# An mLSTM and HGRN2 step on one core: the keys of the four memory heads are turned by VectorE and DMAs instead of TensorE

## The chip, the core and the metric

The kernel runs on one core of a Trainium2 chip. It is one program of some 23,800 instructions over TensorE (PE in the profile; its weight loads are PEld), VectorE (DVE), ScalarE (ACT), GpSimd (POOL) and SyncE (SP, which issues nearly all DMAs). Each engine works through its own instructions in their order and waits for others by semaphores. The metric is the device time of one execution in microseconds (us): the lower, the better.

## What is computed

The reference is one step of a streaming encoder: 512 frames of a new stream and 32 frames of a running one, width 1024, in float32. A projection `x @ w_in` feeds two branches, an mLSTM with four heads of width 512 and an HGRN2 with eight heads of width 128; both are merged by gates and projected out. The part that the change touches is the mLSTM's new matrix memory, a product over time of weighted keys and values, for which the keys are needed with time on the partitions:

```python
qm = jnp.einsum('bthd,hde->bhte', ch, w_qm)
km = jnp.einsum('bthd,hde->bhte', ch, w_km) * (M_HD ** -0.5)
...
w_last = jnp.exp(b[..., -1:] - b + ig - m_last[..., None])
decay = jnp.exp(m_prev[..., -1] - m_last)
C_new = decay[..., None, None] * C + jnp.einsum('bhs,bhse,bhsd->bhed', w_last, v, k)
n_new = decay[..., None] * n + jnp.einsum('bhs,bhsd->bhd', w_last, k)
```

## The kernel before

Every large matrix product is made of three: each float32 operand is split into a high part (`...h`, a rounding copy on ACT) and a low part (`...l`, the rest, a subtraction on DVE), and PE adds up high times high, low times high and high times low. Activations lie with features on the 128 partitions and 544 frames (512 + 32) along the free side; PE takes them in two halves of 272. A weight block of 128x512 arrives by one DMA from SP, is split by one ACT cast (L205) and one DVE subtraction (L206), and then serves 12 matmuls of 128x272, a block.

The heads of the memory run one after the other (loop from L1656): `stage_k` (L970) projects the keys to four tiles `kf` of 128 features by 544 frames and splits them; `stage_q` (L997) does the queries; `stage_scores` (L1025) multiplies both, masks (`dm`) and splits the scores (`sh`, `sl`); then `mchain` (L1119) turns keys and values so that time lies on the partitions, and multiplies them to the new memory. `mchain` is a generator: at each `yield n` the `Pump` (L671) runs n half blocks of the projection `w_in` in between, so that PE has matmuls while ACT and DVE prepare operands. For heads 1 to 3 these come from a pairwise scheme (`Two`) with seven blocks of 12 matmuls: `a11, a12` and so on are plain weights (`wa...`), `s1` to `s4` sums of weights (`ws...`, an addition on DVE at L509 ahead of the split). With heads 1, 2 and 3 the first pair is 20, 24 and 28, and its blocks come in the order a11 (ahead of the scores), a12, s2, s1, s3, then a11 of the next pair, a22 and so on. `Pump.load` (L702) issues the raw weights' DMAs, `Pump.prepare` (L736) writes a block's sums and splits three blocks ahead (AHEAD = 3); with `behind` set, they are issued after the instruction that it names.

In `mchain`, for each of the four blocks b of 128 frames, PE turns the key tiles by four transposes against an identity (L1129) into `kt`; ACT writes the weighted keys' high part `kwh` (L1133), DVE the low part `kwl` (L1134). Three copies of the last stream's 32 frames, `ksm`, are turned the same way (L1144) and give `kws` (L1149, L1151). KTGAP (L45) holds the half blocks ahead of each. The values follow with four transposes per block (`vt`, L1176), split to `vh` (L1179) and `vl` (L1180). For head 3, SP also writes the parts to memory (`kv_d`, L1218).

The order on PE is the order in which the code is written (`manual_schedule`). On ACT, DVE, POOL and SP a scheduler places the instructions ahead of time, by readiness and priority (`high_priority` puts the weighted keys first; `issue_after(x)` keeps an instruction behind x); on the chip that order is fixed, and each queue stops at an instruction that waits.

Of the kernel before, what the change touches and what calls it, by code (L numbers as in the profile page):

```python
# [9 lines left out]
F32 = mybir.dt.float32  # L10
# [4 lines left out]
ALU = mybir.AluOpType  # L15

P = 128
D = 1024
KD = D // P
NS = 32  # L20
NP = 512
T = NS + NP
TH = T // 2
FAR, NEAR = 48, 4
MH = 4
# [19 lines left out]
KTGAP = ((3, 2, 1, 1, 1), (4, 4, 4, 4, 4))  # L45
# [8 lines left out]
SUMSAT = (3,)  # L54
# [30 lines left out]
def hybrid_step(ctx: ExitStack, tc: tile.TileContext, a, o):  # L85
# [585 lines left out]
    class Pump:  # L671


        def __init__(self, todo, staged=False, src=a["w_in"]):
            self.src, self.rawahead = src, RAWAHEAD
            self.done, self.when, self.behind, self.staged = 0, {}, None, staged
# [25 lines left out]
        def load(self, i):  # L702
            b = self.order[i]
            if b[1]:
                need = self.loads.index(b[1][-1]) + 1
                for u, i in self.loads[self.loaded : need + self.rawahead]:
                    self.raw[u, i] = raw_piece(self.src[u][:, i * WP : (i + 1) * WP], f"wi{u}r{i}")
                self.loaded = max(self.loaded, min(need + self.rawahead, len(self.loads)))
# [252 lines left out]

    def triple(src, name, after=None):

        t = small(name, [P, KH, 3, NS], bufs=1)
        for f in range(KH):
            with tc.issue_after(after.ins) if after is not None else nullcontext():
                last = G.tensor_copy(t[:, f], src[f][:, :NS].rearrange("p (o t) -> p o t", o=1).to_broadcast([P, 3, NS]))  # L967
        return t.rearrange("p f o t -> p f (o t)"), last

    def stage_k(h):  # L970

        cs = st8[h]["cs"]
        kf, ks = [], []
        for u in range(2):
            w = st8[h]["wk"][u] if "wk" in st8[h] else weight(a["w_km"][h, u], f"wk{h}{u}", at=in_slots)
            for f in range(2):
# [11 lines left out]
                kf.append(t)  # L988
                kh, kl = slot(f"kh{h}{u}{f}", F32R), slot(f"kl{h}{u}{f}", F32R)
                S.copy(kh[:, :NP], t[:, NS:T])  # L990
                V.tensor_tensor(kl[:, :NP], t[:, NS:T], kh[:, :NP].bitcast(F32), ALU.subtract)
                ks.append((kh, kl))
        ksm, copied = triple(kf, "ksm")
        st8[h].update(kf=kf, ks=ks, ksm=ksm, copied=copied)
# [122 lines left out]
    kv_d = dr.tile([2 * NB, 2, P, VW], F32, name="kv_d")  # L1117

    def mchain(h, pump):  # L1119
# [3 lines left out]
        kf, ksm, wi = t["kf"], t["ksm"], t["wi"]  # L1123
        kw = []
        for b in range(NB):
            yield KTGAP[h > 0][b]
            pt = paux(f"kt{h}{b}")
            for f in range(KH):
                PE.transpose(pt[:, 0, f * P : (f + 1) * P], kf[f][:, NS + b * P : NS + (b + 1) * P], ident)  # L1129
            kh, kl = slot(f"kwh{h}{b}", F32R), slot(f"kwl{h}{b}", F32R)  # L1130
            wc = col[:, 10 + b, h : h + 1]
            with tc.high_priority():
                S.mul(kh[:, :HD], pt[:, 0, :], wc)  # L1133
                low = V.scalar_tensor_tensor(kl[:, :HD], pt[:, 0, :], wc, kh[:, :HD].bitcast(F32), ALU.mult, ALU.subtract)  # L1134
            if h == 0 and b in SUMSAT:
                with tc.issue_after(low.ins):
                    for k in FIRST:
                        xf[k] = xf_sums(k)
                    lower_bounds()
            kw.append((kh, kl))  # L1140
        yield KTGAP[h > 0][NB]
        pt = paux(f"kts{h}")
        for f in range(KH):
            PE.transpose(pt[: 3 * NS, 0, f * P : (f + 1) * P], ksm[:, f], ident)  # L1144

        kws = small("kws", [3 * NS, HD], F32R, bufs=1)
        wc = cols[:, 1, h : h + 1]
        with tc.high_priority():
            S.mul(kws, pt[: 3 * NS, 0, :], wc)  # L1149
            lo = slice(2 * NS, 3 * NS)  # L1150
            V.scalar_tensor_tensor(kws[lo], pt[lo, 0, :], wc[lo], kws[lo].bitcast(F32), ALU.mult, ALU.subtract)  # L1151
# [504 lines left out]
    with tc.manual_schedule(engines={mybir.EngineType.PE}):  # L1656
        for h in range(MH):
# [9 lines left out]
            if h == 0:  # L1667
                col, cols, combo = stage_cols(*rows)
                stage_decay(h)
                lower_bounds = hgrn_bounds(st8[0]["decayed"], st8[0]["masked"])  # L1670
# [525 lines left out]
```

## Time and profile before

| | us |
|---|---|
| median of three runs | 1108.1 (1108.09 to 1108.41) |
| the profiled execution | 1109.5 |
| its span, first to last instruction | 1107.8 |
| PE busy | 1098.2 |
| DVE busy | 920.7 |
| ACT busy | 713.9 |
| POOL busy | 166.8 |
| the DMA engines' share, main queue | 37.4% |

How to read it: PE's busy time is nearly the span, so what PE does not have to do shortens the step, and what PE has to wait for lengthens it, wherever in the step that is. The timeline rows in the next sections give the start (us from the span's start), the duration, the engine, the line, the operation with its output and inputs (buffer numbers left out) and how often; a bracket holds the idle time ahead and what ended it. Since instructions of one engine overlap by their latency, the pitch from one start to the next is the time that one costs in a row of them.

### The profile page before, as it was taken

Reading aid. Unit: us, or ns where it says so; the run is one execution under the profiler, and the core shown is the slowest. Engines: PE = TensorE matmul, PEld = TensorE weight load, DVE = VectorE, ACT = ScalarE, POOL = GpSimd, SP = SyncE. Lnnn points to the kernel's source line nnn. Section 1 sums busy time; section 2 is a strip of 40 time slices with the busy share of each in tenths; the row PEclk is TensorE's granted clock in tenths of the full one; section 3 lists DMA queues with packets and bytes.
Section 4 is the critical chain, followed back from the end, with each engine's and each line's share of the span. In section 5 each row is a group of like instructions: output and inputs, shape, how many; then the busy total and the mean of one; then the engine's idle time right before and its main releaser. Section 6 shows DMA issues by size and latency. Waiting matters only on the chain.

```text
span 1107.8 us, 23790 instructions
## 1 busy us (share of the span) xinstructions
PE 1098.2 (99%) x8825; PEld 1085.8 (98%) x8825; DVE 920.7 (83%) x1977; ACT 713.9 (64%) x1571; POOL 166.8 (15%) x417
## 2 busy tenths in 40 slices
PE   9999999999999999999999999999999999999998
PEld 9999999999999999999999999999999999999998
DVE  6987999676896786986898699999999888789785
ACT  6686656754666555664666478787777776445662
POOL 2212024201010110101200123322323100000000
PEclk9999999999999999999999999999999999999999
DMA  6233225332264132461656322122222353343953
GB/s 223 78 96 107 89 78 183 101 113 99 68 218 163 39 125 103 133 224 53 201 172 207 108 77 84 56 84 74 84 71 75 102 177 114 113 126 104 304 153 120
DMA packets 78044, 135.78 MB, mean 123 GB/s; under 512 B 8804, under 2 KB 16612, under 8 KB 77928
## 3 DMA queue, kind: packets, MB, share of 16 engines
q1 hardware_dynamic: 77760, 134.21, 37.4%
q8 instruction: 69, 1.13, 0.4%
q14 instruction: 47, 0.39, 0.1%
q10 hardware_dynamic: 168, 0.06, 0.0%
HBM read 109.32 MB, written 24.91 MB: 121 GB/s over the span
## 4 chain that ended last, share of the span: by engine, by line
PE 89%; DVE 7%; ACT 2%; issue 1%; DMA 1%; SPq 0%; POOL 0%; DVEq 0%; ACTq 0%
PE d L576 38%; PE ya L230 9%; PE pg L2047 4%; PE yb L230 4%; PE k L230 4%; PE q L230 4%; PE C L1098 3%; PE pl L1770 3%; PE u L356 2%; PE sc L1040 2%; PE v L230 2%; PE nm L1280 2%; PE ple L230 1%; PE d L456 1%; PE ho L1885 1%
## 5 line engine op out<-in xcount | busy, mean ns | idle before, releaser
L593 ACT COPY t<-d 128x272 f32<-128x272 f32 x126 | 47.5, 377 | 5.0 <-PE d L576 4.8
L1791 DVE TENSOR_TENSOR hkq<-hkq,hq 128x288 f32<-128x288 f32 (+1 forms) x96 | 41.5, 439 | 4.9 <-PE pl L1778 1.6
L1726 ACT COPY kmos<-hkq 128x256 f32<-128x256 f32 x56 | 23.9, 427 | 30.4 <-DVE hkq L1791 29.6
L1770 PE MATMUL pl<-hkq,kmos 128*128 128x128 f32 x224 | 38.2, 293 | 1.1 <-ACT kmos L1726 0.7
L802 DVE SCALAR_TENSOR_TENSOR cv<-ub,vec,cv 128x547 f32<-128x547 f32 x48 | 37.1, 782 | 0.4
L1770 PEld LDWEIGHTS pl<-hkq,kmos 128*128 128x128 f32 x224 | 30.9, 190 | 3.9 <-ACT kmos L1726 2.4
L1209 DVE SCALAR_TENSOR_TENSOR c<-c,wi,Cs 128x256 f32<-128x256 f32 (+1 forms) x32 | 15.1, 476 | 19.3 <-PE Cs L1207 19.2
L1098 PE MATMUL C<-vh,kwl 128*128 128x256 f32 x96 | 27.0, 281 | 0.0
L1098 PE MATMUL C<-vl,kwh 128*128 128x256 f32 x96 | 26.9, 280 | 0.0
L1098 PE MATMUL C<-vh,kwh 128*128 128x256 f32 x96 | 26.8, 279 | 0.0
L1348 DVE TENSOR_TENSOR y<-ya,y 128x272 f32<-128x272 f32 x48 | 18.8, 434 | 8.1 <-PE ya L230 8.1
L1806 DVE COPY_PREDICATED at<-lmask,pl 128x256 f32<-128x256 uint8 x56 | 24.9, 445 | 0.0
L1280 PE MATMUL nm<-vh,sh 128*128 128x256 f32 x80 | 22.9, 286 | 0.9 <-ACT y L1291 0.5
L1280 PE MATMUL nm<-vh,sl 128*128 128x256 f32 x80 | 22.5, 282 | 0.0
L1280 PE MATMUL nm<-vl,sh 128*128 128x256 f32 x80 | 22.5, 281 | 0.0
L1110 ACT COPY Co<-C 128x516 f32<-128x516 f32 x12 | 7.1, 590 | 21.0 <-PE C L1098 17.4
L1054 ACT CAST sh<-dm 128x512 fp32r<-128x512 f32 (+3 forms) x16 | 7.3, 459 | 20.4 <-DVE dm L1048 20.4
L967 POOL COPY vsm<-vt 128x96 f32<-128x96 f32 x16 | 7.4, 472 | 86.5 <-ACT vt L604 43.6
L1291 ACT COPY y<-nm 128x516 f32<-128x516 f32 x16 | 9.4, 589 | 16.9 <-PE nm L1280 16.9
L1040 PE MATMUL sc<-q,kh 128*128 128x512 f32 (+3 forms) x80 | 18.6, 321 | 0.1
L795 POOL COPY uo<-ub 128x3 f32<-128x3 f32 x16 | 6.8, 428 | 76.4 <-DVE ub L600 40.8
L1098 PEld LDWEIGHTS C<-vh,kwh 128*128 128x128 f32 x96 | 18.1, 189 | 0.0
(5761 smaller groups left out, 5196.1 us busy)
## 6 DMA issues: line engine op xcount, KB each, us to landing
ya_d<-y SPq DMA_DIRECT2D x32, 272.0 KB, 3.0
y<-ya_d SPq DMA_DIRECT2D x24, 272.0 KB, 3.6
c<-in_C SPq DMA_DIRECT2D x16, 258.0 KB, 3.7
out_Cs<-c SPq DMA_DIRECT2D x16, 258.0 KB, 2.7
out_Cp<-Co SPq DMA_DIRECT2D x15, 258.0 KB, 2.5
x<-in_xT SPq DMA_DIRECT2D x8, 272.5 KB, 4.8
ya<-ya_d SPq DMA_DIRECT2D x8, 272.0 KB, 5.1
h<-in_xT SPq DMA_DIRECT2D x8, 272.0 KB, 2.7
```

The lines of the kernel that those rows point to most:

```text
L230: PE.matmul(both[b][:m, :TH], part(w, off + k * step, m, x), xx[:, half(b)], start=(k == 0 and j == 0), stop=(k == n - 1 and j == 2),)
L576: PE.matmul(ps, ww[:, c], xx, start=(start and k == 0 and j == 0), stop=end, skip_group_check=not start,)
L593: S.copy(t, ps)
L802: last = V.scalar_tensor_tensor(cv[:, :547], ub[:, j : j + 547], vcol(V_CW + 4 * ft + j), cv[:, :547], ALU.mult, ALU.add)
L1040: PE.matmul(pn[:, 0, :n], ks[f][x][:, j * P : (j + 1) * P], qs[f][y][:, NS + j * P : T], start=(f == 0 and i == 0), stop=(f == KH - 1 and ...
L1098: PE.matmul(pn[g], kw[b][x][:, f * P : (f + 1) * P], vv[b][y][:, VS[g]], start=(b == 0 and j == 0), stop=(b == NB - 1 and j == 2),)
L1280: PE.matmul(pn[:, g, VP[g] : VP[g] + VN[g]], st[j][x][:, (i - j) * P : (i - j + 1) * P], vv[j][y][:, VS[g]], start=(j == 0 and q == 0), st ...
L1726: S.copy(km.rearrange("p (n j c) -> p n j c", j=2, c=c), view(kk, HB, ((2 * c, NA // (2 * c)), (c - HB, 2), (1, c))),)
L1770: PE.matmul(pn[:, b * P : (b + 1) * P], km[:, b * P : (b + 1) * P], view(qq, b * P, ((2 * c, P // (2 * c)), (HB + c, 2), (1, c))), start=True,
L1791: V.tensor_tensor(x, x, t, ALU.mult)
L1806: V.copy_predicated(blocks2(at[:, :NA]), twice(lmask[:, li, :P]), blocks2(pn[:, :NA]))
L2047: PE.matmul(ps, part(w, k * P, P, x), xx[:, c], start=(k == 0 and j == 0), stop=(k == KD - 1 and j == 2))
```

## The change

The 80 PE transposes of the keys and of `ksm` are taken out. Instead, DVE turns each `kf` tile in place by squares of 32 by 32 (`V.transpose` over 128x544, new function `turn`), and four DMAs per tile, each of 32 partitions by 17 by 32 numbers, write the squares to their places in a buffer `k_d` in memory, frame by frame; 16 such DMAs per head. From there `mchain` reads four blocks of 128x512 into the slots of `kwl`, and three copies of 32x512 into `kr`. ACT and DVE make `kwh`, `kwl` and `kws` from these in SBUF. All reads and splits are written at once behind the scores, ahead of the first `yield`. For heads 1 to 3, later raw weights are issued behind the last read (`ahead`), and later sums and splits of weights behind the last `kwl` (`behind`). Head 0's turns are written behind its decay. KTGAP keeps the sums of half blocks, 8 and 20, in two parts each; the `xf` sums of head 0 stand behind the first 7 of them. The copies `ksm` are made tile by tile in `stage_k`.

```diff
@@ -42,7 +42,7 @@
 PDGAP = 1
 VGAPS = (0, 0, 0, 0)
 ZN = 3
-KTGAP = ((3, 2, 1, 1, 1), (4, 4, 4, 4, 4))
+KTGAP = ((7, 1), (16, 4))
 VTGAP = ((2, 1, 1, 1, 1), (1, 1, 1, 1, 1), (1, 1, 1, 1, 1), (0, 2, 2, 1, 1))
 GAPS = (20, 20, 20, 14)
 APART = 10
@@ -51,7 +51,6 @@
 FACTORS = 0
 HOLDS = (0,)
 WV1AT = 6
-SUMSAT = (3,)
 FIRST = (0,)
 THEN = (3, 1, 2)
 SLOT = 550
@@ -673,7 +672,7 @@
 
         def __init__(self, todo, staged=False, src=a["w_in"]):
             self.src, self.rawahead = src, RAWAHEAD
-            self.done, self.when, self.behind, self.staged = 0, {}, None, staged
+            self.done, self.when, self.behind, self.ahead, self.staged = 0, {}, None, None, staged
             order, base = [], 0
             for n, e in enumerate(todo):
                 last = todo[n - 1] if n else None
@@ -703,8 +702,9 @@
             b = self.order[i]
             if b[1]:
                 need = self.loads.index(b[1][-1]) + 1
-                for u, i in self.loads[self.loaded : need + self.rawahead]:
-                    self.raw[u, i] = raw_piece(self.src[u][:, i * WP : (i + 1) * WP], f"wi{u}r{i}")
+                with tc.issue_after(self.ahead.ins) if self.ahead is not None else nullcontext():
+                    for u, i in self.loads[self.loaded : need + self.rawahead]:
+                        self.raw[u, i] = raw_piece(self.src[u][:, i * WP : (i + 1) * WP], f"wi{u}r{i}")
                 self.loaded = max(self.loaded, min(need + self.rawahead, len(self.loads)))
 
         def stage(self, n, upto):
@@ -959,18 +959,31 @@
         G.tensor_copy(wi, bc[:, T : T + NS])
         st8[h].update(dj=dj, ds=ds, wi=wi, decayed=decayed, masked=masked)
 
+    def thrice(dst, src):
+
+        return G.tensor_copy(dst, src[:, :NS].rearrange("p (o t) -> p o t", o=1).to_broadcast([P, 3, NS]))
+
     def triple(src, name, after=None):
 
         t = small(name, [P, KH, 3, NS], bufs=1)
         for f in range(KH):
             with tc.issue_after(after.ins) if after is not None else nullcontext():
-                last = G.tensor_copy(t[:, f], src[f][:, :NS].rearrange("p (o t) -> p o t", o=1).to_broadcast([P, 3, NS]))
+                last = thrice(t[:, f], src[f])
         return t.rearrange("p f o t -> p f (o t)"), last
+
+    def turn(dst, f, t):
+
+        V.transpose(t[:, :T], t[:, :T])
+        blocks = dst.rearrange("(n t) e -> t n e", t=NS)
+        for i in range(P // NS):
+            e = f * P + i * NS
+            nc.sync.dma_start(blocks[:, :, e : e + NS], t[i * NS : (i + 1) * NS, :T].rearrange("p (n e) -> p n e", e=NS))
 
     def stage_k(h):
 
         cs = st8[h]["cs"]
         kf, ks = [], []
+        ksm = small("ksm", [P, KH, 3, NS], bufs=1)
         for u in range(2):
             w = st8[h]["wk"][u] if "wk" in st8[h] else weight(a["w_km"][h, u], f"wk{h}{u}", at=in_slots)
             for f in range(2):
@@ -985,13 +998,15 @@
                     read = S.mul(t[:, half(b)], acc[b], HD**-0.5)
                 if u == 0:
                     first = read
-                kf.append(t)
                 kh, kl = slot(f"kh{h}{u}{f}", F32R), slot(f"kl{h}{u}{f}", F32R)
                 S.copy(kh[:, :NP], t[:, NS:T])
                 V.tensor_tensor(kl[:, :NP], t[:, NS:T], kh[:, :NP].bitcast(F32), ALU.subtract)
+                copied = thrice(ksm[:, u * 2 + f], t)
+                if h:
+                    turn(k_d[h], u * 2 + f, t)
+                kf.append(t)
                 ks.append((kh, kl))
-        ksm, copied = triple(kf, "ksm")
-        st8[h].update(kf=kf, ks=ks, ksm=ksm, copied=copied)
+        st8[h].update(kf=kf, ks=ks, ksm=ksm.rearrange("p f o t -> p f (o t)"), copied=copied)
         return first
 
     def stage_q(h, u):
@@ -1115,40 +1130,41 @@
         yield
 
     kv_d = dr.tile([2 * NB, 2, P, VW], F32, name="kv_d")
+    k_d = [dr.tile([T, HD], F32, name=f"k_d{h}") for h in range(MH)]
 
     def mchain(h, pump):
 
         t = st8[h]
 
-        kf, ksm, wi = t["kf"], t["ksm"], t["wi"]
+        wi = t["wi"]
         kw = []
         for b in range(NB):
-            yield KTGAP[h > 0][b]
-            pt = paux(f"kt{h}{b}")
-            for f in range(KH):
-                PE.transpose(pt[:, 0, f * P : (f + 1) * P], kf[f][:, NS + b * P : NS + (b + 1) * P], ident)
             kh, kl = slot(f"kwh{h}{b}", F32R), slot(f"kwl{h}{b}", F32R)
+            raw = kl[:, :HD].bitcast(F32)
+            read = nc.sync.dma_start(raw, k_d[h][NS + b * P : NS + (b + 1) * P, :])
             wc = col[:, 10 + b, h : h + 1]
             with tc.high_priority():
-                S.mul(kh[:, :HD], pt[:, 0, :], wc)
-                low = V.scalar_tensor_tensor(kl[:, :HD], pt[:, 0, :], wc, kh[:, :HD].bitcast(F32), ALU.mult, ALU.subtract)
-            if h == 0 and b in SUMSAT:
-                with tc.issue_after(low.ins):
-                    for k in FIRST:
-                        xf[k] = xf_sums(k)
-                    lower_bounds()
+                S.mul(kh[:, :HD], raw, wc)
+                low = V.scalar_tensor_tensor(kl[:, :HD], raw, wc, kh[:, :HD].bitcast(F32), ALU.mult, ALU.subtract)
             kw.append((kh, kl))
-        yield KTGAP[h > 0][NB]
-        pt = paux(f"kts{h}")
-        for f in range(KH):
-            PE.transpose(pt[: 3 * NS, 0, f * P : (f + 1) * P], ksm[:, f], ident)
-
+        if h:
+            pump.ahead, pump.behind = read, low
+        kr = small("kr", [3 * NS, VW], bufs=1, tag="vs")[:, :HD]
+        for i in range(3):
+            nc.sync.dma_start(kr[i * NS : (i + 1) * NS], k_d[h][:NS, :])
         kws = small("kws", [3 * NS, HD], F32R, bufs=1)
         wc = cols[:, 1, h : h + 1]
         with tc.high_priority():
-            S.mul(kws, pt[: 3 * NS, 0, :], wc)
+            S.mul(kws, kr, wc)
             lo = slice(2 * NS, 3 * NS)
-            V.scalar_tensor_tensor(kws[lo], pt[lo, 0, :], wc[lo], kws[lo].bitcast(F32), ALU.mult, ALU.subtract)
+            V.scalar_tensor_tensor(kws[lo], kr[lo], wc[lo], kws[lo].bitcast(F32), ALU.mult, ALU.subtract)
+        yield KTGAP[h > 0][0]
+        if h == 0:
+            with tc.issue_after(low.ins):
+                for k in FIRST:
+                    xf[k] = xf_sums(k)
+                lower_bounds()
+        yield KTGAP[h > 0][1]
         c0 = [eslot(f"c0{h}{f}") for f in range(KH)]
         for f in range(KH):
             nc.sync.dma_start(c0[f][:, :VW], a["C0"][h, f])
@@ -1667,6 +1683,8 @@
             if h == 0:
                 col, cols, combo = stage_cols(*rows)
                 stage_decay(h)
+                for f, t in enumerate(st8[0]["kf"]):
+                    turn(k_d[0], f, t)
                 lower_bounds = hgrn_bounds(st8[0]["decayed"], st8[0]["masked"])
             low = stage_q(h, 1)
             if h == 0:
```

**ScalarE in head 1, from the queries to the first blocks behind the scores.** `ws320h`, `wa1122h` and `wa2220h` are high parts of weights for the blocks s3, a11 of the next pair and a22; `sh` are the scores' high parts; `t1620` is a copy of block s2's result out of PSUM. Before:

```order
L205 CAST ws320h_3449<-ws320_3447 128x512
L205 CAST wa1122h_3468<-wi22r0_3310 128x512
L1016 CAST qh13_3289<-q1111_3264 128x272
L1013 COPY qf_3140<-q1110_3263 128x32
L1016 CAST qh13_3289<-q1110_3263 128x272
L1022 ACT_TABLE_LOAD
L1022 ACTIVATE silu_3296<-ident_108 1x2
L593 COPY t120_3350<-d200_3334 128x272
L205 CAST wa2220h_3495<-wi21r1_3304 128x512
L1054 CAST sh10_3384<-dm10_2958 128x512
L1054 CAST sh11_3402<-dm11_2959 128x384
L1054 CAST sh21_3368<-dm12_2960 128x256
```

and now, from the scores on:

```order
L1069 CAST sh10_3411<-dm10_2965 128x512
L1069 CAST sh11_3429<-dm11_2966 128x384
L1069 CAST sh21_3395<-dm12_2967 128x256
L1069 CAST sh21_3395<-dm12_2967 128x128
L592 COPY t1620_3538<-d200_3361 128x272
L1147 ACTIVATE kwh10_3474<-kwl10_3475,col_1348 128x512
L1158 ACTIVATE kws_3498<-kr_3494,cols_1350 96x512
L1147 ACTIVATE kwh11_3479<-kwl11_3480,col_1348 128x512
L1147 ACTIVATE kwh12_3484<-kwl12_3485,col_1348 128x512
L1147 ACTIVATE kwh13_3489<-kwl13_3490,col_1348 128x512
L204 CAST ws320h_3503<-ws320_3501 128x512
L204 CAST wa1122h_3522<-wi22r0_3337 128x512
```

The casts of the weights stood ahead of the scores and now stand behind the five weighted-key instructions, and these behind the copy of s2's result.

**VectorE in the same place.** `ql` are the queries' low parts, `vt10` a result of block a12, `ws320` the sum of weights for block s3. Before, ahead of the scores:

```order
L509 TENSOR_TENSOR ws222_3517<-ws122_3515,wi22r0_3310 128x512
L1017 TENSOR_TENSOR ql12_3257<-q1100_3230,qh12_3256 128x272
L1017 TENSOR_TENSOR ql12_3257<-q1101_3231,qh12_3256 128x272
L206 TENSOR_TENSOR ws320l_3450<-ws320_3447,ws320h_3449 128x512
L509 TENSOR_TENSOR ws422_3575<-ws222_3517,wi22r1_3466 128x512
L206 TENSOR_TENSOR wa1122l_3469<-wi22r0_3310,wa1122h_3468 128x512
L1017 TENSOR_TENSOR ql13_3290<-q1111_3264,qh13_3289 128x272
L1017 TENSOR_TENSOR ql13_3290<-q1110_3263,qh13_3289 128x272
L206 TENSOR_TENSOR wa2220l_3496<-wi21r1_3304,wa2220h_3495 128x512
L1048 TENSOR_TENSOR dm10_2958<-sc10_3370,dm10_2958 128x512
```

and now, behind them:

```order
L1070 TENSOR_TENSOR sl21_3396<-dm12_2967,sh21_3395 128x128
L1084 TENSOR_TENSOR dss_3470<-dm12_2967,dss_3470 32x32
L599 TENSOR_TENSOR vt10_3363<-d201_3362,t120_3377 128x272
L1148 SCALAR_TENSOR_TENSOR kwl10_3475<-kwl10_3475,col_1348,kwh10_3474 128x512
L1160 SCALAR_TENSOR_TENSOR kws_3498<-kr_3494,cols_1350,kws_3498 32x512
L1148 SCALAR_TENSOR_TENSOR kwl11_3480<-kwl11_3480,col_1348,kwh11_3479 128x512
L1148 SCALAR_TENSOR_TENSOR kwl12_3485<-kwl12_3485,col_1348,kwh12_3484 128x512
L1148 SCALAR_TENSOR_TENSOR kwl13_3490<-kwl13_3490,col_1348,kwh13_3489 128x512
L508 TENSOR_TENSOR ws320_3501<-wi20r0_3325,wi21r0_3329 128x512
L508 TENSOR_TENSOR ws122_3560<-wi23r0_3343,wi23r1_3345 128x512
L508 TENSOR_TENSOR ws222_3562<-ws122_3560,wi22r0_3337 128x512
L205 TENSOR_TENSOR ws320l_3504<-ws320_3501,ws320h_3503 128x512
```

The sum for s3 was made ahead of these rows (and its low part among them); now the sum stands behind the last `kwl`, and its low part behind two further sums.

**ScalarE in head 0, at the turns of the values.** `vt00` and `vt01` are PE's turned values, of which two can be held at a time; `ws24h` belongs to a later block. Before:

```order
L1133 ACTIVATE kwh03_1638<-kt03_1633,col_1344 128x512
L205 CAST wa124h_2208<-wi4r1_1714 128x512
L837 ACTIVATE z01_1670<-d330_1550 128x272
L1149 ACTIVATE kws_1678<-kts0_1673,cols_1346 96x512
L837 ACTIVATE z01_1670<-d331_1551 128x272
L1326 ACTIVATE c1_840<-c1_840,vec_84 128x544
L1179 CAST vh00_1708<-vt00_1703 128x512
L1163 CAST c0p00_1880<-c000_1681 128x516
L1163 CAST c0p01_1883<-c001_1682 128x516
L1179 CAST vh01_1731<-vt01_1726 128x512
L205 CAST ws24h_2232<-ws24_2230 128x512
```

and now:

```order
L1179 CAST c0p00_1887<-c000_1688 128x516
L1179 CAST c0p01_1890<-c001_1689 128x516
L1147 ACTIVATE kwh02_1584<-kwl02_1585,col_1348 128x512
L204 CAST ws24h_2239<-ws24_2237 128x512
L1147 ACTIVATE kwh03_1589<-kwl03_1590,col_1348 128x512
L1195 CAST vh00_1715<-vt00_1710 128x512
L1195 CAST vh01_1738<-vt01_1733 128x512
```

`vh00`, which frees the turned values' PSUM together with `vl00` on DVE, now stands behind `ws24h` and `kwh03`.

**SyncE in head 3, behind the scores.** `kv_d` is the copy of the weighted keys in memory, `s0` a load of HGRN2 state. Before, the writes to `kv_d` stood among loads of weights:

```order
L1840 DMA s0_10116<-in_S0 128x128
L173 DMA wi45r1_7831<-in_w_in 128x512
L173 DMA wi44r1_7881<-in_w_in 128x512
L1218 DMA kv_d_139<-kwh30_7753 128x512
L1218 DMA kv_d_139<-kwl30_7754 128x512
L173 DMA wi46r0_7960<-in_w_in 128x512
L1218 DMA kv_d_139<-kwh31_7805 128x512
L1218 DMA kv_d_139<-kwl31_7806 128x512
L1218 DMA kv_d_139<-kwh32_7857 128x512
L1218 DMA kv_d_139<-kwl32_7858 128x512
```

and now they share the queue with the reads of turned keys:

```order
L1144 DMA kwl30_7743<-k_d3_143 128x512
L1154 DMA kr_7762<-k_d3_143 32x512 x3
L1144 DMA kwl31_7748<-k_d3_143 128x512
L1234 DMA kv_d_139<-kwh30_7742 128x512
L1234 DMA kv_d_139<-kwl30_7743 128x512
L1858 DMA s0_9693<-in_S0 128x128
L1144 DMA kwl32_7753<-k_d3_143 128x512
L1234 DMA kv_d_139<-kwh31_7747 128x512
L1234 DMA kv_d_139<-kwl31_7748 128x512
L1858 DMA s0_10132<-in_S0 128x128
L1144 DMA kwl33_7758<-k_d3_143 128x512
L1234 DMA kv_d_139<-kwh32_7752 128x512
L1234 DMA kv_d_139<-kwl32_7753 128x512
```

The read of the last block, into `kwl33`, stands behind the writing of `kwl31`.

## The prediction

> **What bounds the kernel now.** I read the page first, for the engine that is never free, then the groups of instructions on PE, then the timeline where the change acts.
>
> ```profile
> PE 1098.2 (99%) x8825; PEld 1085.8 (98%) x8825; DVE 920.7 (83%) x1977; ACT 713.9 (64%) x1571; POOL 166.8 (15%) x417
> PE 89%; DVE 7%; ACT 2%; issue 1%; DMA 1%; SPq 0%; POOL 0%; DVEq 0%; ACTq 0%
> ```
>
> PE is busy for 1098.2 of 1107.8 us and makes up 89% of the chain that ended last. So each microsecond taken off PE is worth one, and each that PE waits costs one; nothing behind a wait is caught up, since PE has no slack to catch up with.
>
> ```profile
> L1129 PE MATMUL kt<-ident,kf 128*128 128x128 f32 x64 | 9.6, 272 | 0.0
> L1144 PE MATMUL kts<-ident,ksm 128*96 128x128 f32 x16 | 2.4, 272 | 0.0
> ```
>
> These are the 80 transposes that go. Their idle time is 0.0: PE never waited for them.
>
> **What goes.** Busy time overlaps in a pipelined engine, so I price a group of four from starts in head 1:
>
> ```profile
> 228.64 0.37 PE L576 MATMUL d<-xh,wa1220h 128*128 128x272 f32 x1
> ...
> 231.57 0.29 PE L576 MATMUL d<-xfh,ws220l 128*128 128x272 f32 x1
> 231.70 0.60 PE L1129 MATMUL kt<-ident,kf 128*128 128x128 f32 x4
> 232.05 0.37 PE L576 MATMUL d<-xfh,ws120h 128*128 128x272 f32 x1
> 232.26 0.29 PE L576 MATMUL d<-xfl,ws120h 128*128 128x272 f32 x1
> 232.39 0.28 PE L576 MATMUL d<-xfh,ws120l 128*128 128x272 f32 x1
> ...
> 233.62 0.29 PE L576 MATMUL d<-xfh,ws320h 128*128 128x272 f32 x1
> ```
>
> From 231.70 to 232.05 are 0.35 us, and the next matmul takes 0.21 instead of 0.13, so a group costs about 0.44. There are 20 groups: **8.8 us** saved, at least 20 x 0.35 = 7.0. The same splits of the keys remain on ACT and DVE.
>
> **What comes in, heads 1 to 3.** The rows of order on ACT and DVE say that block s3 (ws320 in head 1) now gets its weights behind all weighted keys, and these stand behind the copy of s2's result. The durations:
>
> ```profile
> 236.95 0.74 DVE L1134 SCALAR_TENSOR_TENSOR kwl<-kt,col,kwh 128x512 fp32r<-128x512 f32 x1
> 237.61 0.68 DVE L509 TENSOR_TENSOR ws<-ws,wi36r 128x512 f32<-128x512 f32 x1
> 238.21 0.68 DVE L206 TENSOR_TENSOR wa1136l<-wi36r,wa1136h 128x512 fp32r<-128x512 f32 x1
> ```
> ```profile
> 232.35 0.38 ACT L593 COPY t<-d 128x272 f32<-128x272 f32 x1
> 232.63 0.69 ACT L1133 ACTIVATE kwh<-kt,col 128x512 fp32r<-128x512 f32 x1
> ```
> ```profile
> 109.14 0.69 ACT L1133 ACTIVATE kwh<-kt,col 128x512 fp32r<-128x512 f32 x1 [0.51 <-PE kt L1129]
> 109.72 0.61 ACT L205 CAST wa124h<-wi4r 128x512 fp32r<-128x512 f32 x1
> 110.23 0.40 ACT L837 ACTIVATE z<-d 128x272 f32<-128x272 f32 x1
> ```
>
> On DVE a `kwl` costs 0.66 in a row, a sum 0.60; on ACT the copy 0.28, a `kwh` from PSUM 0.58, a cast from SBUF 0.51. A `kwh` from SBUF is in no row; it lies between the last two, and I take 0.57, which the five together move by 0.3 at most. In head 1, on the clock of before: s2 ends at 231.57 + 0.29 = 231.86; the copy runs to 232.2; five instructions of 0.57 bring the end of `kwh13` to 235.15; `kwl13` to 235.85; the sum to 236.55; the cast `ws320h` to 237.2. Without transposes PE asks for it at 233.62 - 0.44 = 233.2, so it waits **4.0**. Its third matmul needs `ws320l`, which stands behind two more sums (236.45 + 2 x 0.60 + 0.7 = 238.35) and is asked for at 237.5: **0.9** more. Head 1: 4.9. Behind it the splits run ahead of PE again, at about 0.6 a piece against 1.48 a block. In head 2 one `kwh` stands ahead of the copy: 4.9 - 0.57 = **4.3**.
>
> Head 3 has SP's queue in the way: the read into `kwl33` is issued behind the write of `kwl31`.
>
> ```profile
> 529.52 0.33 SPq L1218 DMA_DIRECT2D kv_d<-kwl  x1
> ```
> ```profile
> c<-in_C SPq DMA_DIRECT2D x16, 258.0 KB, 3.7
> ```
> ```profile
> DMA to landing us min/median/max: 2.3/4.2/5.5
> ```
>
> Counted from the first matmul behind the scores (228.64 in head 1): the copy ends at 3.5, `kws` and `kwh31` follow to 4.8, `kwl31` to 5.6; its write, a state load and the read are issued at 5.6, 5.95 and 6.3; at 3.7 to landing the data is there at 10.0; `kwh33` ends at 10.75, `kwl33` at 11.45, the sum at 12.15, the cast at 12.8. PE asks at 233.2 - 228.64 = 4.5. It waits 8.3, and 0.9 for the low part: **9.2**, with landings of 2.3 to 5.5 (the extremes of the `kv_d` transfers) 7.8 to 11.0.
>
> **Head 0.** Here `vt02` waits for `vl00`, and this for `kwh03` and `kwl03`.
>
> ```profile
> 113.52 0.41 PE L456 MATMUL d<-xl,wi340h 128*128 128x272 f32 x2
> 113.78 0.41 PE L456 MATMUL d<-xh,wi340l 128*128 128x272 f32 x2
> 114.05 0.66 PE L1176 MATMUL vt<-ident,vt 128*128 128x128 f32 x4
> ```
>
> Five groups earlier, PE wants `vt02` at 114.05 - 2.2 = 111.85. `ws24h`, ahead of `kwh03` on ACT, writes over `wi340h`, whose last use begins at 113.52 - 2.2 = 111.3 and ends at 111.75. Then `ws24h` 0.51, `kwh03` to 112.95; DVE has `ws24l` and a sum in between, so `kwl03` ends at 114.2 and `vl00` at 115.0. PE waits 3.1, and 0.2 at the turn of the last frames: **3.3**. The reads are no later: the last is issued behind matmuls of the scores, and some 60 matmuls at 0.13, 7.5 us, lie between the scores and `vt00`, which covers the longest landing of 5.5.
>
> **What is hidden.** 16 turns of 128x544 come on DVE, an operation in no row; the nearest is an addition of that size:
>
> ```profile
> L399 DVE TENSOR_TENSOR xu<-xh,xl 128x544 f32<-128x544 f32 x4 | 2.8, 705 | 0.0
> ```
> ```profile
> 206.51 0.69 DVE L509 TENSOR_TENSOR ws<-wi21r,wi21r 128x512 f32<-128x512 f32 x1 [1.36 <-DMA wi21r<-in_w_in]
> ...
> 211.59 0.78 DVE L1017 TENSOR_TENSOR q<-q,q 128x272 fp32r<-128x272 f32 x2
> ```
> ```profile
> 212.98 0.41 PE L230 MATMUL q<-cs4h,wq110h 128*128 128x272 f32 x2
> ```
>
> Four add 2.8 us ahead of the first queries' low parts (two, done 212.4), whose PSUM PE wants at 212.98. The sum that moved out gives 0.6 back, and DVE waited 1.4 for a weight at 206.5, so they end near 212.9: nothing, by a hair. At twice 0.7 each of heads 1 to 3 would lose 2.5; a turn below an addition gains nothing. The 64 DMAs that write turned keys must end before the reads. A DMA is 544 pieces of 128 B, 34 on each of 16 engines; nothing like it is in the trace. Bounds:
>
> ```profile
> q1 hardware_dynamic: 77760, 134.21, 37.4%
> ```
> ```profile
> q10 hardware_dynamic: 24, 0.01, 0.9%
> ```
> ```profile
> 203.00:212.00 9.00, 9.00 (x76) 9.00 (x75) 7.45 (x14) 6.26 (x16) 3.49 (x6) 1.00 0.39 125
> 212.00:220.00 8.00, 8.00 (x67) 8.00 (x66) 6.22 (x13) 3.88 (x13) 2.06 (x8) 1.00 0.25 91
> 220.00:232.00 12.00, 12.00 (x88) 11.46 (x87) 7.26 (x18) 5.04 (x11) 1.05 (x4) 1.00 0.08 23
> ```
>
> A mean packet of the main queue takes 0.374 x 16 x 1107.8 / 77760 = 85 ns, at 1726 B: 2.9 us a DMA, the upper end; by bytes alone it would be 0.2, the lower. The small packets that ACT sends (24 in the window from 82 to 86, 0.9% of 16 x 4 us) take 24 ns: 0.8 us a DMA, and I take this nearest row. In head 1 the first turn can start near 203.5; other traffic takes 9 x 0.39 + 8 x 0.25 + 12 x 0.08 = 6.5 us; to land by 232.2 the first read must go by 228.3. So 18.3 us are left for 16 DMAs: up to 1.14 us, or **34 ns a piece**, they cost nothing, and each ns above delays the reads of a head by 0.54.
>
> The Trainium skill ("DMA: Bandwidth & Descriptors", Specifications) says that transfers below 512 B become read-modify-write. The row of small packets shows no such doubling, and no run so far has 128 B pieces; by that rule the time would be that of the dear pieces below, an estimated 1151.
>
> **The sum.** -8.8 + 3.3 + 4.9 + 4.3 + 9.2 = +12.9 on the profiled execution's 1109.5: 1122.4. The median of the runs is 1.4 lower, so I forecast **1121.0**.
>
> **Rivals.** *Hidden or cancelled.* The waits decide below 8.8 in sum, of which the four heads give 21.7. If operations from SBUF ran at half the time of those from PSUM, the place being the five behind the copy, heads 0 to 2 would lose some 1.5 each and head 3, with landings at 2.3, some 5: sum 9.5, no change. If head 3's reads then also passed the writes, 1103. The rows speak against it: 0.60 against 0.66 on DVE, 0.51 against 0.58 on ACT. Faster, 1099 to 1105: 0.10; within 0.2%: 0.06. *Dear pieces.* Doubled to 48 ns, the reads come 14 x 0.54 = 7.6 late in each head: +30, 1151; at 40 ns 1134. 0.12. *The clock falls.* PE's clock was low at the start:
>
> ```profile
> 1.10 3.78 PE L1407 MATMUL warm<-warm 128*128 128x128 f32 x16 [1.10 <-DVE emc L1233]
> 4.85 0.82 PE L356 MATMUL u<-x00h,wf0h 128*128 128x272 f32 x2
> 5.47 0.66 PE L356 MATMUL u<-x00l,wf0h 128*128 128x272 f32 x2
> ...
> 6.51 0.41 PE L356 MATMUL u<-x00l,wf0h 128*128 128x272 f32 x2
> 6.76 0.41 PE L356 MATMUL u<-x00h,wf0l 128*128 128x272 f32 x2
> ```
>
> Pairs go from 0.62 to 0.25 within 5 us of PE's first work. If a long wait brings that back, up to 2.5 us are lost each time: 1123.5 if head 3's 8.3 us does it, 1128.5 if those of heads 1 and 2 do too. The Trainium skill ("TensorE: Matmul & The Clock Gate", Why this matters for your kernels) warns of idle gaps above about 3 us; no row of before shows it in the middle of the step. 0.15. The forecast keeps 0.57, 1115 to 1126.
>
> **Range and chances.** 0.2%, 2.2 us, is about what a measurement here tells from no change. Faster 0.10, same 0.06, slower 0.84. The range, 1106 to 1138, leaves out most of the faster case and pieces above 42 ns.
>
> **What would show it.** PE waits before ws320, ws324 and ws328, for ACT's cast, of about 4.0, 3.4 and 8.3, and for DVE 0.9 each; 3 us at `vt02` in head 0; ACT idle behind the scores until s2's end, then five keys in a row. Reads landing after s2's end, with ACT waiting for DMA at `kwh10`, mean dear pieces; matmuls at a pitch above 0.13 behind a wait, the clock. No wait at these blocks would make the prediction wrong.

## The result, and the profile after

| | median, us | lowest to highest, us | runs |
|---|---|---|---|
| kernel before | 1108.64 | 1108.09 to 1109.47 | 6 |
| changed kernel | 1134.61 | 1133.85 to 1137.14 | 6 |

The ratio is 1.0238 (95% interval 1.0225 to 1.025): the change costs 26.0 us. The profiled execution of the changed kernel took 1137.14 us, 2.5 above its median, and the one of the kernel before 1109.5, 0.8 above, so sums read from the two traces may stand a little above the medians.

First the page of the changed kernel: busy time by engine, the granted clock of PE in 40 slices of the span (tenths, 9 is 90% or more), and the new DMAs (KB each, median us from issue to landing).

```profile
PE 1099.9 (97%) x8745; PEld 1086.9 (96%) x8745; DVE 929.6 (82%) x1993; ACT 714.9 (63%) x1571; POOL 171.9 (15%) x417
PEclk9999899989999989999899999999999999999999
k_d<-kf SPq DMA_DIRECT2D x64, 68.0 KB, 2.1
kwl<-k_d SPq DMA_DIRECT2D x16, 256.0 KB, 3.2
```

PE has 80 instructions less, and yet 1.7 us more of busy time than before. Without the transposes it should have 1098.2 - 8.8 = 1089.4, so the rest became 10.5 us dearer. The 8.8 is the estimate from starts, so this is rough. The clock shows dips in four slices, one for each head. The DMAs are quick.

Next PE's waits in the changed kernel (us in total, times, longest).

```profile
PE d L575 <- ACT ws328h L204: 8.1, 1, 8.1
PE vt L1192 <- DVE vl L1196: 7.7, 2, 7.2
PE d L575 <- ACT ws320h L204: 4.5, 1, 4.5
PE d L575 <- ACT ws324h L204: 3.7, 1, 3.7
...
PE d L575 <- DVE ws320l L205: 0.8, 1, 0.8
...
PE d L575 <- DVE ws324l L205: 0.6, 1, 0.6
...
PE d L575 <- DVE ws328l L205: 0.5, 1, 0.5
```

These are the waits that were forecast, at the blocks that were named: 18.2 us in heads 1 to 3. Head 0's wait is the 7.2 of the second row, at `vt02`, and much larger than its term of 3.3; the other 0.5 of that row arises in head 1, at the turns of the values. The timeline of ACT in head 1 shows how one arises:

```profile
236.96 0.39 ACT L592 COPY t<-d 128x272 f32<-128x272 f32 x1 [2.95 <-PE d L575]
237.24 0.73 ACT L1147 ACTIVATE kwh<-kwl,col 128x512 fp32r<-128x512 f32 x1
237.87 0.71 ACT L1158 ACTIVATE kws<-kr,cols 96x512 fp32r<-96x512 f32 x1
238.48 1.93 ACT L1147 ACTIVATE kwh<-kwl,col 128x512 fp32r<-128x512 f32 x3
242.27 0.62 ACT L204 CAST ws320h<-ws 128x512 fp32r<-128x512 f32 x1 [1.86 <-DVE ws L508]
```

ACT idles 2.95 us for s2's end, runs five keys in a row, none of which waits for a DMA, and then waits 1.86 for DVE, which has its own five low parts and a sum to do. What PE does behind that wait was not in the sum:

```profile
242.94 0.39 PE L575 MATMUL d<-xfh,ws320h 128*128 128x272 f32 x1 [4.53 <-ACT ws320h L204]
...
244.22 0.59 PE L575 MATMUL d<-xfh,ws320l 128*128 128x272 f32 x1 [0.76 <-DVE ws320l L205]
244.62 0.43 PE L575 MATMUL d<-xfh,ws320h 128*128 128x272 f32 x1
244.84 0.43 PE L575 MATMUL d<-xfl,ws320h 128*128 128x272 f32 x1
...
250.42 0.29 PE L575 MATMUL d<-xfh,wa2220l 128*128 128x272 f32 x1
```

From 244.62 to about 250 the pitch, from one start to the next, is 0.225 us instead of 0.125. The view by stretches gives the granted clock as its third number from the end; here are stretches behind the waits of heads 0 to 3 in the changed kernel (the last begins within the wait), and one after the recovery in head 1 (third row):

```profile
119.00:122.00 3.00, 3.00 (x15) 3.00 (x15) 3.00 (x9) 0.70 (x2) 0.00 (x0) 0.50 0.30 113
246.00:249.00 3.00, 3.00 (x15) 3.00 (x15) 2.82 (x5) 0.39 (x1) 0.00 (x0) 0.50 0.23 87
251.00:254.00 3.00, 3.00 (x26) 3.00 (x25) 2.57 (x5) 1.85 (x5) 0.55 (x1) 1.00 0.36 120
397.00:401.00 4.00, 3.43 (x14) 3.11 (x15) 4.00 (x7) 2.63 (x6) 0.00 (x0) 0.51 0.53 166
553.00:559.00 6.00, 4.02 (x16) 3.71 (x17) 5.83 (x11) 3.70 (x7) 0.00 (x0) 0.50 0.63 217
```

15 matmuls in 3 us at a clock of 0.50, 26 at 1.00. Below, "offset" is the start of one and the same matmul in two traces, subtracted. The first matmul of block wa1172, behind all four heads, gives the offset of the changed kernel from before, one row from each trace:

```profile
616.76 0.29 PE L576 MATMUL d<-xh,wa1172h 128*128 128x272 f32 x1
```
```profile
642.38 0.29 PE L575 MATMUL d<-xh,wa1172h 128*128 128x272 f32 x1
```

It is 25.6, and still 25.5 at PE's last matmul (1103.81 before, 1129.27 now): what PE loses is lost in the heads. The two spans differ by 27.6; the other 2.2 us lie behind PE's last matmul, where the kept traces differ among themselves (3.9 to 6.2 us in all thirteen), and no run says how much of that is the change.

### The profile page after: what moved, and what is told of

Same layout as the page of the kernel before. It is cut to its first block, busy times and chain, and to the rows that moved or that the text cites. A ratio compares the mean times of both kernels' runs of the same rounds, so it can differ in the third digit from the quotient of the medians.

```text
span 1135.4 us, 23787 instructions
## 1 busy us (share of the span) xinstructions
PE 1099.9 (97%) x8745; PEld 1086.9 (96%) x8745; DVE 929.6 (82%) x1993; ACT 714.9 (63%) x1571; POOL 171.9 (15%) x417
## 3 DMA queue, kind: packets, MB, share of 16 engines
q1 hardware_dynamic: 116480, 143.65, 39.6%
## 4 chain that ended last, share of the span: by engine, by line
PE 90%; DVE 5%; ACT 2%; issue 1%; DMA 1%; SPq 0%; DVEq 0%; ACTq 0%
PE d L575 38%; PE ya L229 8%; PE pg L2065 4%; PE yb L229 4%; PE q L229 4%; PE k L229 4%; PE C L1113 4%; PE sc L1055 3%; PE pl L1788 2%; PE nm L1296 2%; PE u L355 2%; PE v L229 2%; PE d L455 2%; DVE ws L508 1%; PE ple L229 1%
## 5 line engine op out<-in xcount | busy, mean ns | idle before, releaser
L794 POOL COPY uo<-ub 128x3 f32<-128x3 f32 x16 | 14.7, 918 | 33.1 <-DVE ub L601 23.4
L1055 PE MATMUL sc<-q,kh 128*128 128x512 f32 (+3 forms) x80 | 18.4, 320 | 0.0
L1192 PE MATMUL vt<-ident,vt 128*128 128x128 f32 x64 | 10.6, 293 | 7.7 <-DVE vl L1196 7.7
```

Source lines behind the costliest of these rows:

```text
L1055: PE.matmul(pn[:, 0, :n], ks[f][x][:, j * P : (j + 1) * P], qs[f][y][:, NS + j * P : T], start=(f == 0 and i == 0), stop=(f == KH - 1 and ...
```

## Experiments

All kernels of a group ran beside the kernel before, whose median was 1108.7 to 1109.0 in each. Edits are against the changed kernel unless the text says otherwise.

### One suspect at a time: the clock, the hold, the writes, head 0

`fill`: matmuls that do nothing useful, ahead of ws320, ws324 and ws328, so that PE is busy where it would idle.

```diff
+FILL = (0, 33, 26, 60)
...
-        yield KTGAP[h > 0][0]
+        def fill(ps):
+            for _ in range(FILL[h]):
+                PE.matmul(ps, xs[0][0][:, :P], xs[0][0][:, :TH], start=True, stop=True)
...
+        if h:
+            yield 6
+            fill(paux(f"fill{h}")[:, 0, :TH])
+            yield 10
...
```

> 33, 26 and 60 matmuls of 128x272, whose results nobody reads, stand on TensorE ahead of blocks ws320, ws324 and ws328, where the changed kernel waits 4.5, 3.7 and 8.1 us. Theory clock: the matmuls at a pitch of 0.225 us behind each wait are TensorE at half its clock, brought about by the wait itself; with the waits filled the clock stays at 1.00 in heads 1 to 3, and some 3 us a head come back: about 1126 us instead of 1134.6, with the weights arriving no earlier. Rival: the slow matmuls come from the turned keys' DMAs and reads beside them, or from bunched splits; then the pitch stays at 0.225 and the time at 1133 to 1137.

Measured 1132.73, ratio 1.0215 (1.0198 to 1.0232). PE's timeline in head 1 of this kernel:

```profile
238.24 4.30 PE L1164 MATMUL fill<-xh 128*128 128x272 f32 x33
242.94 0.39 PE L576 MATMUL d<-xfh,ws320h 128*128 128x272 f32 x1 [0.41 <-ACT ws320h L205]
...
244.22 0.39 PE L576 MATMUL d<-xfh,ws320l 128*128 128x272 f32 x1 [0.76 <-DVE ws320l L206]
244.45 0.29 PE L576 MATMUL d<-xfh,ws320h 128*128 128x272 f32 x1
244.58 0.29 PE L576 MATMUL d<-xfl,ws320h 128*128 128x272 f32 x1
```

ws320 starts at the same 242.94, its low part keeps its wait of 0.76, and the pitch behind is 0.13, from 244.45 on. The offset from the changed kernel falls by 2.7, 2.6 and 2.0 us behind the three waits: 7.3 us are the price of the slow clock in heads 1 to 3. That it is the idleness which lowers the clock is shown, and this was expected. The time fell less than expected (1126): PE then waits at other places (0.21 and 0.75 at head 2's transposes of the values, 0.38 and 0.64 in head 3's products), and behind them the offset has given back 1.2 and 2.2. The median gained 1.9. So 7.3 us is what the slow clock takes in this kernel, not what the kernel gains without it.

`nobehind`: weights are no longer held behind the last key (`pump.ahead = read` alone is set). 

> Later weight splits are no longer issued behind the last turned key (behind is not set; ahead stays). Theory queue: ACT and DVE make the weights of s3 ahead of the scores again, the waits at ws320, ws324 and ws328 (18 us with their low parts) and the half clock behind them (some 9 us) go: 1107 to 1112 us, head 0's wait of 7.2 left. Rival: the turning itself (DVE turns, 128 B pieces, reads) is what costs in heads 1 to 3; then the time stays above 1125 us.

Measured 1125.84, ratio 1.0155 (1.0139 to 1.017). The waits at ws320, ws324 and ws328 are gone, yet only 8.8 us came back. This expectation fell. By its number the rival holds; the next group takes its cause, the turning, apart from the rest, and the group after that shows what the time is.

`kvlate`: SP issues the writes of head 3's keys behind its last read.

```diff
-                    nc.sync.dma_start(kv_d[b, i, :, :HD], kw[b][i][:, :HD].bitcast(F32))
+                    with tc.issue_after(read.ins):
+                        nc.sync.dma_start(kv_d[b, i, :, :HD], kw[b][i][:, :HD].bitcast(F32))
```

> In head 3 the writes of weighted keys to kv_d are issued behind the last read of turned keys. Theory queue: the wait at ws328 falls from 8.1 to about 4 us (as in heads 1 and 2), the half clock behind it stays: 1130 to 1131 us. Rival: the read is late for another reason (late turns of head 3, or DMA load in that place); then the wait stays near 8 us and the time at 1134 us.

Measured 1131.02, ratio 1.0201 (1.0186 to 1.0216); PE's wait at ws328 in that kernel:

```profile
PE d L575 <- ACT ws328h L204: 3.7, 1, 3.7
```

Head 3 now waits as long as head 2 (3.7 in both kernels): its extra 4.4 us came from the writes ahead of the read on SP. In the changed kernel two `kwh` of head 3 wait 1.8 and 2.6 us on ACT for their reads; in this one none does.

`h0pe`: head 0's keys by PE transposes as before, heads 1 to 3 as changed. 

> Head 0 is turned by TensorE as before the change, heads 1 to 3 as changed. Theory queue and clock: the wait of 7.2 us at vt02 and 2.7 us of half clock go, five groups of transposes of 0.44 us come back: -7.7, about 1127 us. Rival: head 0's late vt02 comes from later weights that wait for slots, not from the turned keys; then the wait remains in part and the time stays above 1131 us.

Measured 1128.64, ratio 1.018 (1.0165 to 1.0195), 6.0 below the changed kernel: the wait of 7.2 at `vt` is gone, and 1.7 less came back than expected.

### Are the turns themselves free?

`turnonly` is the kernel before with the turns, their 48 DMAs and 12 reads put into heads 1 to 3, while PE still transposes the keys:

```diff
+        if h:
+            for f, t in enumerate(kf):
+                turn(k_d[h], f, t)
...
+        for b in range(NB if h else 0):
+            raw = slot(f"kwl{h}{b}", F32R)
+            kw.append(raw)
+            nc.sync.dma_start(raw[:, :HD].bitcast(F32), k_d[h][NS + b * P : NS + (b + 1) * P, :])
```

> The kernel before with the turns of heads 1 to 3 put in (12 transpositions on VectorE, 48 DMAs that write the turned keys, 12 reads of them), while the 80 transposes on PE and the splits stay where they were. It leaves out the right keys: PE transposes what VectorE has turned already, so the output is not the reference's. Theory (the turns and their pieces are hidden, the time comes from where the splits stand): 1108 to 1110, no new wait. Rival (turns and small pieces load VectorE or the queue, and after's small waits come from that): 1113 or more, with new waits for VectorE's low parts behind the scores in each head.

Measured 1110.73, ratio 1.0015 (1.0006 to 1.0024): about 1.7 us for three heads, a little above the range expected, and far from the rival. No wait of PE in the heads is longer than 0.8, but "no new wait" held only roughly: 0.28 and 0.39 at head 1's turns of the values, 0.19 at head 2's and 0.76 at ws244 in head 3 are new, while one of 0.73 in head 3 shrank to 0.38. That is 1.3 us in sum. In the changed kernel a turn takes 742 ns (mean of 16), where the prediction took 0.7, and a DMA of 544 pieces lands in 2.1 us. The main queue's share rose from 37.4% of 1107.8 to 39.6% of 1135.4 us, on 16 engines some 565 us more of engine time; divided by 34,816 pieces that is some 16 ns a piece, with the reads counted in, where the prediction took 24. Dear pieces would have shown as late reads: in the changed kernel no `kwh` of heads 0 to 2 waits for a DMA, and the two in head 3 that do wait behind writes (`kvlate`). Whether these pieces become read-modify-write, as the Trainium skill ("DMA: Bandwidth & Descriptors", Specifications) says of transfers below 512 B, no run here shows.

### Where the splits stand, and the two holds

`spread`: head 0 by PE, the writes behind the reads, and in heads 1 to 3 the reads at once but one split every four half blocks, as before. Weights stay held behind the last read, and are not held behind the last key.

```diff
...
+            for b, (kh, kl) in enumerate(kw):
+                yield 4
+                raw, wc = kl[:, :HD].bitcast(F32), col[:, 10 + b, h : h + 1]
+                with tc.high_priority():
+                    S.mul(kh[:, :HD], raw, wc)
...
```

> The changed kernel with head 0 by PE as before, the writes of the last head's keys behind the reads, and the splits of heads 1 to 3 not at once but one every four blocks, as before, from keys that were read at once. Theory (the place of the splits makes the waits, the turned keys themselves are worth 16 groups of 0.44 us): 1108.7 - 7.0 = 1102, at most 1104, no wait at ws320, ws324, ws328. Rival (VectorE's and the queue's load remains and PE waits at other places): 1107 or more.

`best1`: head 0 by PE, the writes behind the reads, no hold behind the keys; the one behind the reads stays. 

> The changed kernel with head 0 by PE as before, the writes behind the reads, and the pump not held behind the keys; the splits of heads 1 to 3 are still issued at once, and where they fall is left to the priorities. Theory: the sum of the parts, nobehind's 1125.8 less 6.0 for head 0 and up to 3.8 for the wait at head 3's output, 1116 to 1120, with small waits behind the scores. Rival (the parts share a cost that goes only when all are gone): 1104 or less.

`neither`: neither hold, otherwise as changed.

```diff
-        if h:
-            pump.ahead, pump.behind = read, low
```

> The changed kernel without both holds of the pump: the pieces of W_in are not held behind the reads of the keys, nor the splits behind the last key. Theory (the hold behind the keys made the waits; the other one orders only the issue of reads that land long before they are needed): as with the one hold taken away, 1125.8, within 2. Rival (the hold behind the reads starves the weights' loads): 1122 or less, the small waits for wa122, wa123 and ws236 gone.

`noahead`, run later, keeps the hold behind the keys alone. 

> The changed kernel with the hold behind the last key kept and the one behind the reads taken away. Theory (the hold behind the keys alone makes ws320, ws324 and ws328 wait; wi22's second half is issued after 242 whatever the other hold does, since its buffer comes free with the late splits): 1133 to 1136, as the change. Rival (the reads' hold adds to it as it did without the other one, 14 us): 1125 or less.

| | hold behind the reads | not held behind the reads |
|---|---|---|
| hold behind the keys | 1134.61 (the change) | 1135.77 (noahead) |
| not held behind the keys | 1125.84 (nobehind) | 1111.76 (neither) |

`neither` has a ratio of 1.0027 (1.0018 to 1.0036), `noahead` 1.0241 (1.0227 to 1.0255), `spread` 0.9991 (0.9981 to 1.0), `best1` 1.0059 (1.0042 to 1.0075). I had expected `neither` to be like `nobehind`; it is 14.1 us faster, so the theory that the hold behind the reads orders only the issue was wrong. `noahead` came as expected; `best1`, with 1115.14, is a little below its range, the sum of the parts, and far from its rival; `spread`, with 1107.64, fell in its rival's range. With both holds taken away 22.8 of the 26.0 us are gone, with head 0 still turned; either hold alone costs, 24.0 and 14.1, and together they cost no more than the one behind the keys.

How the hold behind the reads costs, in head 1: SP's queue in `nobehind`, and then in `neither` (a row of several DMAs runs from the first issue to the last):

```profile
225.01 8.16 SPq L1144 DMA_DIRECT2D kwl<-k_d  x3
233.22 0.42 SPq L172 DMA_DIRECT2D wi22r<-in_w_in  x1
```
```profile
224.65 0.42 SPq L1144 DMA_DIRECT2D kwl<-k_d  x1
225.12 0.43 SPq L172 DMA_DIRECT2D wi22r<-in_w_in  x1
```

The last reads have to wait for their buffers, and the weights of wi22 stand behind them: 8.1 us later than without the hold. On ACT, whose order is fixed ahead of time, the cast of these weights stands behind all four keys in `nobehind`, but behind two in `neither`:

```profile
245.25 0.73 ACT L1147 ACTIVATE kwh<-kwl,col 128x512 fp32r<-128x512 f32 x1
245.87 0.61 ACT L204 CAST wa1222h<-wi22r 128x512 fp32r<-128x512 f32 x1
```
```profile
241.96 0.73 ACT L1147 ACTIVATE kwh<-kwl,col 128x512 fp32r<-128x512 f32 x1
242.59 0.61 ACT L204 CAST wa1222h<-wi22r 128x512 fp32r<-128x512 f32 x1
```

The weights were there by about 236 in `nobehind` too (233.22 and 2.9 to landing), so it is the order on ACT that makes the cast late; that the scheduler chose this order because it reckoned with the late load is my reading, and no run tests it. PE then waits 1.8 us for wa1222's low part, and at the same place 0.7 in head 2 (wa1226) and 1.8 in head 3 (wa1230). Comparing the two kernels' offsets, `nobehind` loses 3.5, 3.0 and 5.3 us to `neither` in heads 1, 2 and 3, and 4.2 more at head 3's output (16.0 in sum; the two profiled executions are 16.2 apart, the medians 14.1). At that output PE waits three times (0.92, 0.41, 0.27) within 2.5 us, and the clock falls again, as the stretches of `nobehind` show (the waits, and behind them):

```profile
593.00:595.50 2.50, 0.90 (x5) 0.51 (x5) 2.24 (x7) 2.50 (x5) 0.00 (x0) 1.00 0.00 0
595.60:598.60 3.00, 3.00 (x16) 3.00 (x15) 1.93 (x4) 1.51 (x3) 0.00 (x0) 0.50 0.28 93
```

But such waits do not always do it. In `best1` PE waits at the same place 1.12, 0.21 and 0.27, again 1.6 in sum, with the same busy time, and the clock stays:

```profile
583.80:586.30 2.50, 0.91 (x5) 0.52 (x6) 2.40 (x7) 2.50 (x5) 0.00 (x0) 1.00 0.05 17
586.30:589.30 3.00, 3.00 (x26) 3.00 (x26) 2.67 (x6) 1.96 (x5) 0.00 (x0) 1.00 0.27 92
```

`spread` shows that splits in their old places, with reads at once, wait nowhere long; its offset falls by 2.2 in head 2 behind the scores, five groups of 0.44. But its offset also rises: 1.3 at the queries of head 1, where PE waits 0.8 for their low parts (the place that the prediction called covered by a hair), 2.1 around ws236 and the values' turns in head 1 (a wait of 1.2), and 1.7 at the values' turns of head 3 (a wait of 1.4). So it gives 1107.64, not 1102.

### Head 0's wait, and the version without holds and without it

Head 0 of the changed kernel, where `vt02` waits for `vl00`: ACT, then DVE, then PE.

```profile
107.34 0.69 ACT L837 ACTIVATE z<-d 128x272 f32<-128x272 f32 x2 [2.49 <-PE d L455]
107.91 0.62 ACT L204 CAST wa124h<-wi4r 128x512 fp32r<-128x512 f32 x1
108.42 0.76 ACT L1342 ACTIVATE c<-c,vec 128x544 f32<-128x544 f32 x1
109.07 0.72 ACT L1147 ACTIVATE kwh<-kwl,col 128x512 fp32r<-128x512 f32 x1
...
114.77 0.62 ACT L204 CAST ws24h<-ws 128x512 fp32r<-128x512 f32 x1 [2.10 <-DVE ws L508]
115.29 0.72 ACT L1147 ACTIVATE kwh<-kwl,col 128x512 fp32r<-128x512 f32 x1
```
```profile
112.06 1.29 DVE L1180 TENSOR_TENSOR c0p<-c,c0p 128x516 fp32r<-128x516 f32 x2
...
113.99 0.69 DVE L508 TENSOR_TENSOR ws<-ws,wi4r 128x512 f32<-128x512 f32 x1
...
117.07 0.74 DVE L1148 SCALAR_TENSOR_TENSOR kwl<-kwl,col,kwh 128x512 fp32r<-128x512 f32 x1
117.73 1.28 DVE L1196 TENSOR_TENSOR vl<-vt,vh 128x512 fp32r<-128x512 f32 x2
```
```profile
118.55 1.09 PE L1192 MATMUL vt<-ident,vt 128*128 128x128 f32 x4 [7.25 <-DVE vl L1196]
```

The first key stands behind `z`, which waits for PE, and two more instructions; `ws24h` waits 2.10 for DVE's two sums, of which the second is shown; they come after the low parts of `kwh00`, `kws` and `kwh01` and the two of `c0p`. `kwh03`, `kwl03` and `vl00` follow `ws24h`.

`nei_gap6`: `neither` with five half blocks (30 matmuls) more ahead of the values' turns.

```diff
-KTGAP = ((7, 1), (16, 4))
+KTGAP = ((7, 6), (16, 4))
```

> The kernel without both holds, with head 0's keys turned as in the change, and its transposes of the values put five blocks (30 matmuls of 128x272, 3.75 us) later. The order on ACT and VectorE up to kwl03 stays. Theory (kwl03 comes too late for vt02 by a fixed time, because kwh00 to kwh03 stand behind z and wa124h on ACT): the wait at vt02 falls from 7.2 to about 3.5, 1111.8 - 3.75 = 1108. Rival (the wait is for something that moves with the transposes, the copies vh and vl of the values): the wait stays at 6 to 7 and the time at 1111 to 1112.

Measured 1109.29, ratio 1.0004 (0.9995 to 1.0013), with this wait:

```profile
118.91 0.63 PE L1190 MATMUL vt<-ident,vt 128*128 128x128 f32 x4 [3.51 <-DVE vl L1194]
```

The wait fell from 7.2 to 3.5 and `vt02` starts at 118.91, where it started at 119.23 in `neither`: `kwl03`'s chain keeps its time, whatever PE does between the keys and the turns of the values. The rival fell. The time gained 2.5 where 3.75 were expected; at the output's transposes `yt` PE now waits 1.7 us more for `c`.

`nei_h0pe`: neither hold, and head 0 by PE. 

> The kernel without both holds, and head 0's keys by PE as before. Theory (the time lies in the two holds and in head 0's wait, and nowhere else): 1111.8 less head 0's 5 to 6, 1106 to 1107, below before's 1108.7, with no wait above 1.5 us behind the scores of any head. Rival (head 0's wait only hides one that comes later): 1109 or more.

Measured **1104.77**, ratio 0.9966 (0.9954 to 0.9979): below both kernels, and a little below the range expected. The offset from before falls by 2.2 behind the scores of each of the heads 1 to 3 (five groups of 0.44), gives back some of it at the values' turns of heads 1 and 2, and is -4.36 behind the heads; the granted clock over the span is 0.999.

## Why the prediction was too low

The sign was right, the size was not: +12.9 was forecast, +26.0 came. Two steps failed: the clock, put at nothing, and the size of head 0's wait. That 1134.6 lies within the stated range is luck: its upper part was there for dear pieces, which did not come. By its own steps:

- **What goes, -8.8.** Supported: `spread` gains 2.2 in head 2 for five groups, `nei_h0pe` 2.2 in each of three heads.
- **Heads 1 to 3, 4.9 + 4.3 + 9.2 = 18.4.** Right, place by place: 5.3, 4.3 and 8.6, in sum 18.2. `kvlate` shows the part of SP's queue in head 3: 4.4.
- **Head 0, 3.3.** The mechanism was right, `vt02` waiting for `vl00` behind `kwh03`, and the size wrong: 7.2. The step that failed is "`ws24h` ... writes over `wi340h`, whose last use ... ends at 111.75. Then `ws24h` 0.51, `kwh03` to 112.95". The buffer was not what came last: `ws24h` waited until 114.77 for DVE's sums. I had walked back along ACT's queue, but not along DVE's behind each of its entries. The term is 3.9 us too low.
- **What is hidden.** Turns, pieces and reads cost next to nothing, as taken: `turnonly` puts them at 1.7 us for three heads. The chance of 0.12 for dear pieces was not needed.
- **The clock, 0 in the sum.** This is the larger part. The rival named it, with "up to 2.5 us" a wait, and it was given 0.15; it came true behind all four waits. `fill` measures 2.7, 2.6 and 2.0 for heads 1 to 3. For head 0, from `vt02` to block wi350 it was 119.05 - 114.05 = 5.00 before, with a wait of 0.40 in it, and is 125.42 - 118.55 = 6.87 now, 1.9 more. In sum 9.2.

```profile
119.05 0.41 PE L456 MATMUL d<-xh,wi350h 128*128 128x272 f32 x2
```
```profile
125.42 0.41 PE L455 MATMUL d<-xh,wi350h 128*128 128x272 f32 x2
```

Together: -8.8 + 7.2 + 18.2 + 9.2 = 25.8, against an offset of 25.6 in the trace and 26.0 in the medians. That is closer than the terms are: waits below 1 us that came or went are not in it (0.5 at head 1's turns of the values is new; 0.4 and 0.5 at head 0's output and 0.7 at head 3's turns of the values are gone).

The rule in the Trainium skill ("TensorE: Matmul & The Clock Gate", Why this matters for your kernels), that idle gaps above about 3 us bring the slow clock back, agrees with these traces: gaps of 3.5 to 8.1 us did, one of 1.8 in `nobehind` did not. It does not cover the three short waits of `nobehind`, behind which the clock fell as well. The rows of before showed the price of the slow clock, at the start of the step, but none showed that a wait brings it back: the chance was too small, the price about right.

What stays open: what decided between `nobehind` and `best1`, whose three short waits are alike while only one clock fell, and why the scheduler placed the late weights' casts behind the keys.

## What to carry to other kernels

A wait of an engine that has no slack costs more than its length where it is long enough to lower the clock: here, in head 1, 4.5 us cost 7.2. Moving work off the bottleneck paid here only where its followers on the other engines were not forced into one row; the same turned keys gave +2.4% with their splits in one row ahead of the weights, and -0.3% without the holds and with head 0 left alone. Before an order is forced on one queue, ask what in that queue waits for a buffer: everything behind it is late by that wait, and the fixed orders of other engines follow.

## What the runs showed of the hardware

- The low clock is half by the grant (0.50), with a pitch of 0.225 against 0.125, 1.8 times as long; it lasts 5.5 us behind the wait in head 1 while PE works without pause (244.62 to about 250.1), and then ends at once.
- Whether the clock falls does not hang on the length of one wait alone: a gap of 1.76 us left it at full speed, but three waits of 1.6 us in sum, within 2.5 us in which PE was busy for 0.90, halved it for 3 us in `nobehind`. In `best1` the same sum with 0.91 busy did not.
- In-place turns of 128x544 in squares of 32 take DVE 742 ns, like an addition of that size, and the DMAs that write 544 pieces of 128 B (68 KB) land in 2.1 us; the reads in whole rows, of 256 KB, take 3.2.
